# Low parts of the projections' weights by an adding transfer instead of a subtraction

## The chip, the cores and the metric

The kernel runs on one core of a Trainium2 chip. The metric is the device time of one execution in microseconds; the time of a kernel is the median of its runs. The core has five engines that work side by side, each with its own queue of instructions in a fixed order: TensorE (PE, matmuls; PEld is its loading of weights), VectorE (DVE), ScalarE (ACT), GpSimd (POOL) and SyncE (SP, which only issues transfers here). Transfers (DMA) between HBM and the on-chip memory are issued from SP, ACT or POOL and carried out by 16 transfer engines. An instruction waits in its queue until the semaphores it needs are set, and everything behind it waits too.

## The reference

Two layers on a sequence of 1024 tokens of width 1024, all in float32. The first layer is a mixer followed by a mixture of experts, the second one is attention and pooling followed by a gated network. The change lies in the mixer's input projection:

```
h = rmsnorm(x, norm_g)
proj = h @ w_in                      # 1024 x 1024 by 1024 x 2048
y_hyena = hyena_mixer(proj[..., :1536], ...)     # short convolution, long convolution by FFT
y_fourier = fourier_mixer(proj[..., 1536:])
y = head_rmsnorm(concatenate([y_hyena, y_fourier]), mix_g)
x = x + y @ w_out
```

## The kernel before

**Matrix products in three parts.** TensorE multiplies in a rounded float32 (`F32R`). To keep the accuracy, each operand is split into a high part, the value rounded by writing it as `F32R`, and a low part, the value less the high part. `mm3` then issues three matmuls into one PSUM tile: high by high (L61), high by low (L62) and low by high (L64). `split` makes the parts: ScalarE casts (L51), VectorE subtracts (L52).

**The input projection.** `w_in` is cut into 16 column tiles of 128 outputs, each 128 partitions by 8 by 128 values (4 KB per partition, 512 KB). `weight(c)` loads tile `c` into `wr` by a transfer from SP (L110) and splits it into `wh` and `wl`. The pool `pw` has two buffers of each of these, so a tile can be loaded and split while TensorE works on the one before, and a split into a buffer waits until the matmuls of the tile two before are done. `proj(c)` runs 48 matmuls per tile: two halves of 512 tokens, 8 pieces of the inner dimension, three matmuls each. The third matmul of each piece needs `wl`. Its outputs are PSUM tiles named `proj` (or `tp`, for the tile that is called with `pair`).

**Order of the stage.** The tiles come in the order 12, 13, 14, 15 (the Fourier half, `proj_u`, whose results are scaled on VectorE at L181), then 4, 8, 5, 9, then 6, 10, 7, 11, then 0, 1, 2, 3 (`conv`). Tile 12 is loaded and split first of all, between the pieces of the input `x`, which `split` with a scale turns into `xh` (L54) and `xl` (L55). Between the projections stand: the filter's small network (`mlp`, L298, L304), the norm (matmuls with `ones`, L165), the filter's spectrum (`filter_spectrum`, twice, GpSimd's part of it at L408), the data's spectrum (`data_spectrum`, twice) and its product with the filter (`filtered`, twice; VectorE at L542 to L547, GpSimd at L543 and L544, loads of `K` from SP at L540). `conv` scales the projection from PSUM into `up` on VectorE (L197), which also frees the PSUM tile for a later projection, and does the short convolution on ScalarE (L198) and VectorE (L199, L200). GpSimd clears two columns of `up` (L194, L195).

**GpSimd's transfers.** GpSimd issues, early on, four transfers of 1 MB, the transform constants `fwh` and `fwl` (L150). They are held back until the input has landed: a copy of two values of the last piece of `x` into each of the two tiles stands ahead of them (L148).

The instructions of an engine don't stand strictly in the order of the source: the framework that builds the kernel puts them in an order by their place in the source and by when it takes them to be ready.

Of the kernel before, what the change touches and what calls it, by code (L numbers as in the profile page):

```python
# [13 lines left out]
AF = mybir.ActivationFunctionType  # L14
# [4 lines left out]
MUL, ADD, SUB = ALU.mult, ALU.add, ALU.subtract  # L19
# [25 lines left out]
def f32(ap):  # L45
    return ap.bitcast(F32)

def split(nc, hi, lo, src, scale=None):

    if scale is None:  # L50
        nc.scalar.copy(hi, src)  # L51
        nc.vector.tensor_sub(lo, src, f32(hi))  # L52
    else:
        nc.scalar.activation(hi, src, AF.Copy, scale=scale)  # L54
        nc.vector.scalar_tensor_tensor(lo, src, scale, f32(hi), op0=MUL, op1=SUB)  # L55
# [27 lines left out]
def mixer(g):  # L83
    nc, tc, I = g.nc, g.tc, g.I
# [23 lines left out]
    def weight(c):  # L108
        wr = pw.tile([P, 8, P], F32, name="wr", tag="wr")
        nc.sync.dma_start(out=wr, in_=I["w_in"][c])  # L110
        wh = pw.tile([P, 8, P], F32R, name="wh")
        wl = pw.tile([P, 8, P], F32R, name="wl")
        split(nc, wh, wl, wr)
        return wh, wl

    def proj(c, w=None, pair=False):
        wh, wl = w or weight(c)
        if pair:
            both = ps.tile([P, 2, 512], F32, name="tp")
        out = []  # L120
        for h in range(2):
            sl = slice(h * 512, h * 512 + 512)
            pt = both[:, h] if pair else psA.tile([P, 512], F32, name="proj")
            for k in range(8):
                mm3(nc, [pt], wh[:, k], wl[:, k], [xh[k][:, sl]], [xl[k][:, sl]], k == 0, k == 7)
            out.append((pt, sl))
        return out

    keep_warm(g, psA.tile([P, 4, P], F32, name="proj"), g.ones, g.ones[:, None, :].to_broadcast([P, 4, P]), 5)
    with tpool(tc, name="kst", bufs=2) as pk:  # L130
# [11 lines left out]
        xs = x_in(0)  # L142
        xs = [next(xs), xs]
        w12 = weight(12)
        xs = [xs[0], *xs[1], *x_in(4)]
        for t, nm in ((g.fwh, "c_fwh"), (g.fwl, "c_fwl")):

            nc.gpsimd.tensor_copy(t[0:1, 0, :, 0, 0], xs[3][0:1, 1, 0:2])  # L148
            for q in range(2):
                nc.gpsimd.dma_start(out=t[:, :, q].rearrange("p r a b -> p r (a b)"),  # L150
                                    in_=I[nm][:, q].rearrange("r p c -> p r c"))
# [1995 lines left out]
```

## Time and profile before

| | us |
|---|---|
| median of 3 runs | 2517.74 |
| lowest and highest run | 2515.53, 2522.01 |
| the profiled execution, its own time | 2524.19 |
| its span, first to last instruction | 2522.4 |

The profile is of one execution. Its times count from the start of the span. In the page the busy time of an engine is given with its share of the span. A line of a timeline gives start, duration, engine, line of the kernel, operation, tiles and shapes; the square brackets at its end say how long the engine had been idle before it, and what ended that. Matmuls are pipelined, and their ends are modelled: the distance between two starts says more than the duration. The granted clock of TensorE (PEclk) was 0.978 of full speed in the mean.

### The profile page before, as it was taken

What the parts mean: (1) busy time and instruction counts of PE and PEld (TensorE: products, weight loads), DVE (VectorE), ACT (ScalarE), POOL (GpSimd) and SP (SyncE); (2) the same over time, 40 slices, a digit from 0 to 9 for tenths busy, and PEclk for the clock granted to TensorE, in tenths of its full rate; (3) what the DMA queues carried; (4) which work ended last, traced back from release to release, by engine and by line L of the source; (5) the groups of instructions that cost most, each with busy time, mean ns of one, the idle gap of its engine ahead of it and who ended that gap; (6) DMA issues with size and microseconds to landing.
All of it is one profiled execution on the core that took longest, in us unless ns stands there. A gap on an engine that the chain in (4) does not pass through costs nothing.

```text
span 2522.4 us, 30742 instructions
## 1 busy us (share of the span) xinstructions
PE 2396.0 (95%) x11367; PEld 1885.5 (75%) x11367; DVE 1783.4 (71%) x2440; ACT 1288.8 (51%) x1702; POOL 596.7 (24%) x552
## 2 busy tenths in 40 slices
PE   9999688989999999997999999998989999999998
PEld 6887575867777777766888777776878888887786
DVE  7757686459999998886512665666488787777666
ACT  6322145337777777776312765662354444444443
POOL 1124442122222223412101011101113443442001
PEclk9999898989999999998999999998999999999999
DMA  6313645279999999965122111126213322326765
GB/s 230 120 57 127 211 140 207 107 255 368 371 368 370 371 363 358 361 237 198 34 76 97 55 42 53 61 67 233 82 70 101 109 105 92 113 97 235 229 199 184
DMA packets 121666, 451.16 MB, mean 179 GB/s; under 512 B 17510, under 2 KB 20520, under 8 KB 95658
## 3 DMA queue, kind: packets, MB, share of 16 engines
q1 hardware_dynamic: 87136, 346.94, 38.6%
q0 software_dynamic: 31776, 100.73, 12.2%
q8 instruction: 90, 1.47, 0.2%
q10 hardware_dynamic: 2602, 1.51, 0.2%
q14 instruction: 62, 0.51, 0.1%
HBM read 382.79 MB, written 74.71 MB: 181 GB/s over the span
## 4 chain that ended last, share of the span: by engine, by line
PE 70%; DVE 6%; ACT 4%; issue 3%; DMA 2%; POOL 1%; SPq 0%; DVEq 0%; POOLq 0%; ACTq 0%
PE proj L61 12%; PE proj L64 11%; PE proj L62 11%; PE w_gate L62 2%; PE w_up L61 2%; PE w_up L62 2%; PE w_up L64 2%; PE w_gate L64 2%; PE w_gate L61 2%; PE yd L61 2%; PE yd L62 2%; PE yd L64 2%; PE pmix L64 1%; PE pmix L61 1%; PE pmix L62 1%
## 5 line engine op out<-in xcount | busy, mean ns | idle before, releaser
L1000 DVE TENSOR_TENSOR wlo<-raw,whi 128x2048 fp32r<-128x2048 f32 (+1 forms) x195 | 438.6, 2255 | 47.5 <-ACT whi L999 43.6
L999 ACT CAST whi<-raw 128x2048 fp32r<-128x2048 f32 (+1 forms) x195 | 365.6, 1880 | 74.2 <-PE w_up L64 29.5
L61 PE MATMUL proj<-hh,wthi 128*128 128x512 f32 (+1 forms) x576 | 214.3, 376 | 1.3 <-ACT wthi L51 0.9
L62 PE MATMUL proj<-hl,wthi 128*128 128x512 f32 (+1 forms) x576 | 215.3, 375 | 0.2
L64 PE MATMUL proj<-hh,wtlo 128*128 128x512 f32 (+1 forms) x576 | 214.5, 374 | 0.0
L1058 POOL DMA_INDIRECT x1d<-y,tab x32 | 105.9, 3310 | 229.6 <-ACT whi L999 173.7
L52 DVE TENSOR_TENSOR wtlo<-wraw,wthi 128x1024 fp32r<-128x1024 f32 (+1 forms) x44 | 49.5, 1126 | 130.1 <-ACT wthi L51 129.7
L1751 POOL TENSOR_TENSOR vg<-vg 128x1024 f32<-128x1024 f32 x22 | 66.5, 3025 | 258.9 <-ACT vg L1750 258.9
L62 PE MATMUL proj<-fdbl,fdah 128*128 128x512 f32 x308 | 121.9, 396 | 4.5 <-DVE fdbl L52 4.4
L61 PE MATMUL proj<-fdbh,fdah 128*128 128x512 f32 x308 | 121.6, 395 | 3.7 <-DVE fo L1872 2.9
L61 PEld LDWEIGHTS proj<-hh,wthi 128*128 128x128 f32 x576 | 108.3, 190 | 19.2 <-ACT wthi L51 1.3
L62 PEld LDWEIGHTS proj<-hl,wthi 128*128 128x128 f32 x576 | 108.7, 189 | 17.9 <-DVE hl L52 0.7
L64 PEld LDWEIGHTS proj<-hh,wtlo 128*128 128x128 f32 x576 | 108.7, 189 | 17.3
L64 PE MATMUL proj<-fdbh,fdal 128*128 128x512 f32 x308 | 121.0, 393 | 0.0
L61 PE MATMUL proj<-xh,wh 128*128 128x512 f32 x240 | 96.9, 405 | 11.5 <-DVE up L197 10.6
L62 PE MATMUL w_gate<-wlo,xh 128*96 128x512 f32 x256 | 102.0, 398 | 2.4 <-DVE wlo L1000 2.3
L77 POOL TENSOR_TENSOR rs_o<-rs_v,mhalf 128x1 f32<-128x1 f32 x48 | 38.2, 796 | 271.0 <-DVE ssf L1869 178.6
L62 PE MATMUL w_up<-wlo,xh 128*96 128x512 f32 x256 | 101.2, 395 | 0.0
L61 PE MATMUL w_gate<-whi,xh 128*96 128x512 f32 x256 | 100.9, 394 | 0.2
L61 PE MATMUL w_up<-whi,xh 128*96 128x512 f32 x256 | 100.9, 394 | 0.0
L64 PE MATMUL w_gate<-whi,xl 128*96 128x512 f32 x256 | 100.6, 393 | 0.0
L64 PE MATMUL w_up<-whi,xl 128*96 128x512 f32 x256 | 100.5, 392 | 0.0
(544 smaller groups left out, 6781.9 us busy)
## 6 DMA issues: line engine op xcount, KB each, us to landing
raw<-in_w_gate SPq DMA_DIRECT2D x64, 1024.0 KB, 19.1
raw<-in_w_down SPq DMA_DIRECT2D x63, 1024.0 KB, 21.5
raw<-in_w_up SPq DMA_DIRECT2D x62, 1024.0 KB, 21.5
wraw<-in_w_up SPq DMA_DIRECT2D x44, 512.0 KB, 3.5
draw<-in_w_down SPq DMA_DIRECT2D x88, 256.0 KB, 3.7
draw<-ad SPq DMA_DIRECT2D x77, 256.0 KB, 2.8
wraw<-in_w_in SPq DMA_DIRECT2D x32, 512.0 KB, 3.6
ad<-as POOLq DMA_DIRECT2D x44, 256.0 KB, 2.3
```

The lines of the kernel that those rows point to most:

```text
L52: nc.vector.tensor_sub(lo, src, f32(hi))
L61: nc.tensor.matmul(outs[i], lhsT=wh, rhs=xh[i], start=start, stop=False, skip_group_check=onto)
L62: nc.tensor.matmul(outs[i], lhsT=wh, rhs=xl[i], start=False, stop=False, skip_group_check=onto)
L64: nc.tensor.matmul(outs[i], lhsT=wl, rhs=xh[i], start=False, stop=stop, skip_group_check=onto)
L77: nc.gpsimd.tensor_tensor(o, v, g.mhalf if n == 1 else g.mhalf.to_broadcast([P, n]), op=ALU.pow)
L999: g.nc.scalar.copy(hi[:, sl], raw[:, sl])
L1000: eng.tensor_sub(lo[:, sl], raw[:, sl], f32(hi[:, sl]))
L1058: return nc.gpsimd.indirect_dma_start(out=g.x1d, out_offset=bass.IndirectOffsetOnAxis(ap=rows, axis=0), in_=y.rearrange("p a b -> p (a b)" ...
L1751: nc.gpsimd.tensor_mul(va, va, ga)
```

## The change

In `weight(c)` the split stays as it is for tile 12. For the 15 other tiles the high part is made by the same cast on ScalarE, and the low part in two steps: ScalarE writes the negated weights into `wl`, rounded as the high part is, and then a transfer issued from GpSimd reads the raw weights from HBM again and adds them to what stands in `wl`. The sum is the raw value less the high part.

```
         wh = pw.tile([P, 8, P], F32R, name="wh")
         wl = pw.tile([P, 8, P], F32R, name="wl")
-        split(nc, wh, wl, wr)
+        if c == 12:
+            split(nc, wh, wl, wr)
+        else:
+
+            nc.scalar.copy(wh, wr)
+            nc.scalar.activation(wl, wr, AF.Copy, scale=-1.0)
+            nc.gpsimd.dma_start(out=wl, in_=I["w_in"][c], accum_op=ADD)
         return wh, wl
```

## Rows read from the trace of the kernel before

**Rows 1.** The page: busy time by engine; the last chain's shares by engine.
```profile
PE 2396.0 (95%) x11367; PEld 1885.5 (75%) x11367; DVE 1783.4 (71%) x2440; ACT 1288.8 (51%) x1702; POOL 596.7 (24%) x552
...
PE 70%; DVE 6%; ACT 4%; issue 3%; DMA 2%; POOL 1%; SPq 0%; DVEq 0%; POOLq 0%; ACTq 0%
```

**Rows 2.** Windows: length, busy PE, PEld, DVE, ACT, POOL; PEclk, DMA share, GB/s.
```profile
30.00:45.00 15.00, 15.00 (x63) 11.53 (x62) 10.69 (x23) 12.09 (x17) 0.00 (x0) 1.00 0.76 235
45.00:120.00 75.00, 74.72 (x461) 66.05 (x460) 60.87 (x115) 27.33 (x48) 7.73 (x6) 1.00 0.36 124
120.00:160.00 40.00, 40.00 (x178) 32.40 (x178) 22.57 (x21) 9.28 (x9) 7.18 (x9) 1.00 0.27 92
```

**Rows 3.** Waits of PE, 30 to 160 us: total us, times, longest.
```profile
PE hp L370 <- ACT fwoh L51: 0.2, 1, 0.2
```

**Rows 4.** Waits of PE, 180 to 290 us.
```profile
PE proj L61 <- DVE up L197: 10.6, 7, 3.7
```

**Rows 5.** Tile view of wh: ns min/median/max, first and last start us.
```profile
L51 ACT CAST wh<-wr x16: 1029/1047/1057, 9.7 to 258.6; 128x1024 fp32r<-128x1024 f32 x16
L52 DVE TENSOR_TENSOR wl<-wr,wh x16: 1215/1221/1719, 11.6 to 268.0; 128x1024 fp32r<-128x1024 f32 x16
```

**Rows 6.** Tile view of wl, 180 to 290 us.
```profile
L52 DVE TENSOR_TENSOR wl<-wr,wh x6: 1215/1218/1719, 187.3 to 268.0; 128x1024 fp32r<-128x1024 f32 x6
```

**Rows 7.** Timeline of VectorE, 186 to 196 us.
```profile
194.74 0.68 DVE L197 TENSOR_TENSOR up<-proj,rb 128x512 f32<-128x512 f32 x1
```

**Rows 8.** Timeline of ScalarE, 0 to 130 us.
```profile
21.89 1.13 ACT L54 ACTIVATE xh<-xr,g 128x1024 fp32r<-128x1024 f32 x1
...
24.94 1.03 ACT L51 CAST wh<-wr 128x1024 fp32r<-128x1024 f32 x1
...
28.88 1.03 ACT L51 CAST wh<-wr 128x1024 fp32r<-128x1024 f32 x1
```

**Rows 9.** DMA view: issues by line, KB each, median us from issue to landing.
```profile
wr<-in_w_in SPq DMA_DIRECT2D x16, 512.0 KB, 4.0
...
xb<-h2d,tab POOLq DMA_INDIRECT x32, 9.0
x1d<-y,tab POOLq DMA_INDIRECT x32, 10.5
```

**Rows 10.** Timeline of ScalarE, 125 to 320 us.
```profile
132.53 1.06 ACT L51 CAST wh<-wr 128x1024 fp32r<-128x1024 f32 x1 [8.76 <-PE proj L62]
133.50 1.25 ACT L198 ACTIVATE vc<-up,cw 128x1024 f32<-128x1024 f32 x1
```

**Rows 11.** Timeline of TensorE, 140 to 150 us.
```profile
144.23 0.40 PE L64 MATMUL proj<-xh,wl 128*128 128x512 f32 x1
```

**Rows 12.** Tile views of fwh and fwl: the constants' issues and landings.
```profile
L150 POOL DMA_DIRECT2D fwh<-in_c_fwh x2: 778/849/920, 21.5 to 22.5; - x2
...
DMA to landing us min/median/max: 5.8/6.7/7.6
...
L150 POOL DMA_DIRECT2D fwl<-in_c_fwl x2: 775/778/782, 23.2 to 23.9; - x2
...
DMA to landing us min/median/max: 9.9/12.0/14.1
```

**Rows 13.** Timeline of TensorE, 27 to 35 us.
```profile
29.92 0.39 PE L64 MATMUL tp<-xh,wl 128*128 128x512 f32 x1
30.15 0.39 PE L61 MATMUL tp<-xh,wh 128*128 128x512 f32 x1
...
32.48 1.88 PE L165 MATMUL tp<-xr,ones 128*128 128x512 f32 x4
```

**Rows 14.** Timeline of TensorE, 268 to 273 us.
```profile
268.13 0.50 PE L61 MATMUL proj<-xh,wh 128*128 128x512 f32 x1 [3.74 <-DVE up L197]
...
269.23 0.63 PE L62 MATMUL proj<-xl,wh 128*128 128x512 f32 x1
...
271.79 0.63 PE L62 MATMUL proj<-xl,wh 128*128 128x512 f32 x1
```

## The prediction

> **What bounds the kernel now.** The page first: TensorE is busy 95% of the span and carries 70% of the chain that ended last [rows 1]. The shares of that chain add up to 86%, since it isn't followed back to the start; the missing 14%, some 350 us, are the beginning, with the stage that the diff touches (the mixer's projections, 0 to 290 us). I therefore read that stage by its windows and waits. From 30 to 160 us TensorE has work in 129.7 of 130 us [rows 2], and its waits in these 130 us come to 0.2 us [rows 3]. So here a stall of TensorE is not made up later: every microsecond moves all that follows. From 180 to 290 us it is different: there TensorE waits seven times, 10.6 us in all, for VectorE's `up` (L197), which empties a projection's PSUM bank [rows 4]. VectorE is a candidate for a gain there, and there alone.
>
> **What is removed.** Fifteen of the sixteen subtractions `wl <- wr, wh` on VectorE, 1.22 us each [rows 5]: 18.3 us. From 30 to 160 us TensorE waits for none of VectorE's work, so there the removal is worth nothing; the cover is TensorE's own stream of matmuls. From 180 to 290 us it counts where a subtraction stands in VectorE's queue ahead of an L197 for which TensorE waits. Six of the fifteen fall there (column tiles 7, 11 and 0 to 3), the first at 187.3 us [rows 6], ahead of the L197 at 194.74 [rows 7]. Not every one precedes a wait, and in between VectorE waits for transfers and for GpSimd, which swallows the time. Bounds: nothing, and all 10.6 us. I take two subtractions' worth, a gain of 2 us, nearer the low end because six subtractions are 7.3 us at the most.
>
> **What is added on ScalarE.** Fifteen negated copies, between 1.05 us (the cast of a weight [rows 5]) and 1.13 us (an activation with a scale on the same shape [rows 8]): 16 us. ScalarE is busy 27 of 75 us from 45 to 120 and 9 of 40 after [rows 2], so there it costs nothing but latency: the low part begins a copy later. In the first 45 us ScalarE is nearly full, and two copies push the squares and the filter's sines back by 1 us each; TensorE's own stream covers that from 30 us on, and I put it at zero (bounds 0 and 2).
>
> **What is added as transfers.** Fifteen transfers of 512 KB from HBM, adding into `wl`, issued from GpSimd. A low part was there after 1.05 us of cast and 1.22 us of subtraction; it now needs the cast, the negation, GpSimd's turn and a whole transfer. The trace shows no adding transfer into SBUF. Nearest rows: a plain load of the same 512 KB lands in 4.0 us; the adding scatter of 384 KB into HBM (L1058, 96 rows of 4 KB) lands in 10.5, where the gather of as much lands in 9.0 under the same traffic [rows 9]. So the adding itself is worth some 1.5 us, and a landing lies between 4.0 and 10.5; I take 5.5, near the plain load, since the gather shows where most of the scatter's time comes from.
>
> **Most loads have room for it.** A weight is loaded while TensorE still works on the one before. Column tile 8 is typical of the tight ones: cast at 132.53 [rows 10], first use of the low part at 144.23 [rows 11], a lead of 11.7 us. Needed: 1.05 + 1.13, another 1.25 if the convolution's activation goes between [rows 10], and 5.5 from issue to landing: 7.7 to 8.9 us. It fits with 3 us in hand. Some issues will meet GpSimd in a long operation ahead of them in its queue; and while an issue waits for its negation, GpSimd's own work stands behind it (the products of L543 and L544, for whose results VectorE's L546 and then L197 wait). For both together I add 1 us (lower bound 0). That the raw tile `wr` now comes free at the negation and not at the subtraction moves the next plain load by about nothing, and the 7.9 MB read a second time find transfer engines that are 27 to 36% busy from 45 to 160 us [rows 2]. The upper bound is the scatter's 10.5: 12.7 to 13.9 us, late by 1.0 to 2.2 us on each of about six loads with a lead like this, say 9 us.
>
> **The second load has none.** This is column tile 13, the first of the fifteen. Its cast starts at 24.94 [rows 8], so the negation is done at 27.0 at the earliest, and near 30 if it falls where the next weight's cast was (28.88). GpSimd's queue is the trouble: just ahead, at 21.5 to 23.9 us, it issues four transfers of 1 MB, the constants fwh and fwl. Start and time to landing [rows 12] give landings at 21.5 + 5.8 = 27.3, then 22.5 + 7.6 = 30.1, 23.2 + 9.9 = 33.1 and 23.9 + 14.1 = 38.0 us: one behind the other, 2.8 to 4.9 us per MB, 3.6 in the mean. The new transfer stands behind them in the same queue, so its 0.5 MB lands at 38.0 + 1.8 = 39.8 at best, and with the adding's 1.5 at 41.3; I take 41.0 (upper bound 43, if it moves its bytes twice as well). TensorE wants this low part at 29.92 [rows 13]. Behind that matmul in its queue stand the rest of the tile's 48 and then all of the filter's. The stall is 41.0 - 29.92 = 11.1 us.
>
> What could be done in the meantime: the four matmuls for the norm at 32.48 (1.88 us [rows 13]), if they are put ahead of the waiting one: a credit of 0 to 1.9, I take 1.0. And the clock: after a wait of 3.74 us at 268.13, the seven matmuls from 269.23 to 271.79 start 0.43 us apart [rows 14], where 0.23 is usual at the full clock (29.92 to 30.15 [rows 13]): 1.4 us lost. A wait of 11 us should lose no less: 1.5.
>
> By the Trainium skill's page "DMA: Bandwidth & Descriptors", section on the anatomy of one DMA on the SWDGE (gpsimd) path, a transfer takes about 2.0 us plus its bytes by 436 GB/s, an estimate of 3.2 us for 512 KB; from an issue at 27 to 30 us that would leave a stall of under 4 us. The constants' four transfers here don't agree with it: it gives 4.4 us for 1 MB, and they took 5.8 to 14.1.
> The Trainium skill's page "Collectives: The Full Stack", where it explains why ReduceScatter is half of AllGather, says that an add in the transfer's path needs two source reads per byte delivered; by that the 1.8 us would be 3.6, the landing 41.6 and the sum 0.6 larger, an estimate. No row here shows it for SBUF.
>
> **Sum.** 11.1 - 1.0 + 1.5 for the second load, + 1.0 for the others, - 2.0 for VectorE: + 10.6 us. The profiled execution took 2524.19 us (span 2522.4), 6.5 above the median of the runs, 2517.74; the difference goes on the median: 2528 us. About 0.3% (7.6 us) is what can be told from no change here.
>
> **The rivals.**
> A (forecast): the second low part waits behind the constants. Own range: a stall of 9.9 less 1.9 of credit, less 4 on VectorE, gives + 4; 13.1 + 1.5 + 2 gives + 17: 2522 to 2535.
> B, the transfer is hidden anyway: it lands some 5 us after its issue because the transfer engines take it between the constants' pieces, or because it is issued ahead of them, at about 32 us. Stall 2, VectorE 2 back: 2518. For it: the order in which a queue's pieces run on the engines isn't in the rows, only the landings are. Against: those four come strictly in order of issue.
> C, adding is slow everywhere: at the scatter's 10.5 us each tight load is late too, + 11 and 9 more: 2538. For it: the only adding rows. Against: the gather beside it is nearly as slow, so most of it is traffic, which this stage has less of.
> D, VectorE's queue was the bound from 180 on: without the subtractions each L197 comes before TensorE asks, and the 10.6 us vanish. It decides once the stall at the second load is under 10.6; with one of 2 it gives - 8.6, 2509 us. For it: seven waits with one releaser [rows 4]. Against: six subtractions hold 7.3 us of VectorE, not 10.6.
>
> **How the numbers follow.** A 0.56, B 0.22, C 0.14, D 0.08. Of A, some 0.44 lies above + 7.6 us; with C that is 0.58 slower; the rest of A and B, 0.34, is no difference; D, 0.08, is faster. The range reaches from D's upper part to C: 2512 to 2541.
>
> **What would show it.** Right: TensorE's first `xh,wl` matmul of the second tile near 41 instead of 29.92 us with a wait of about 10 us for the transfer into `wl`, a low clock right after, and everything from 45 to 160 us unchanged but moved. The adding transfers issued later land in 5 to 6 us, and TensorE doesn't wait for them. The seven waits for L197 shrink by about 2 us. Wrong: the second transfer landing before 35 us, or its constants issued behind it; or waits for `wl` at six or more tiles.

## The result, and the profile after

The changed kernel takes 2551.98 us (median of 4 runs, 2548.36 to 2557.0), the kernel before beside it 2517.53: a ratio of 1.0125, interval 1.0109 to 1.0142. The forecast was 2528 with a range that ended at 2541, so the time lies outside it, on the side that was forecast. The profiled execution took 2551.96 us, its span is 2550.2 (before: 2522.4). In the lines below, those behind the edit have moved by six: the cast is L117, the negation L118, the adding transfer L119, and `up` is L203 instead of L197.

The page's busy times by engine first; they answer to [rows 1]:

```profile
PE 2393.4 (94%) x11367; PEld 1883.9 (74%) x11367; DVE 1760.8 (69%) x2425; ACT 1303.4 (51%) x1717; POOL 606.3 (24%) x567
```

VectorE's 15 subtractions are gone (2440 to 2425 instructions), ScalarE has 15 copies more, TensorE's work is the same. The loss is waiting. The windows that answer to [rows 2], with the same columns:

```profile
30.00:45.00 15.00, 7.13 (x18) 4.81 (x19) 8.02 (x19) 12.77 (x18) 1.80 (x2) 0.71 1.08 300
45.00:120.00 75.00, 69.06 (x377) 58.56 (x377) 50.73 (x99) 29.29 (x48) 7.65 (x7) 0.97 0.41 122
120.00:160.00 40.00, 40.00 (x226) 34.68 (x225) 16.70 (x25) 9.22 (x11) 9.43 (x11) 1.00 0.51 134
```

TensorE was busy for 15.00, 74.72 and 40.00 us in these stretches [rows 2]; it now has 7.13, 69.06 and 40.00. The waits of TensorE from 30 to 160 us (engine, line, what it waited for: total us, times, longest), which came to 0.2 us [rows 3]:

```profile
PE tp L64 <- DMA wl<-in_w_in: 6.9, 1, 6.9
PE hp L376 <- DVE eo L388: 2.5, 1, 2.5
PE hp L376 <- DVE fwol L52: 2.2, 1, 2.2
PE hp L376 <- ACT fwoh L51: 1.2, 1, 1.2
PE tp L171 <- DVE xr L169: 1.1, 1, 1.1
```

The first is the second load, as forecast. The next three were not: TensorE waits for the filter's spectrum (`hp`), which has no part in the change. From 180 to 290 us, against 10.6 us in seven waits [rows 4]:

```profile
PE proj L61 <- DVE up L203: 7.7, 3, 4.5
PE proj L64 <- DMA wl<-in_w_in: 2.4, 2, 1.3
```

**The second load.** The timelines of TensorE, and of GpSimd ahead of it, at column tile 13:

```profile
40.72 0.79 PE L64 MATMUL tp<-xh,wl 128*128 128x512 f32 x1 [6.87 <-DMA wl<-in_w_in]
42.16 0.63 PE L64 MATMUL tp<-xh,wl 128*128 128x512 f32 x1
...
46.00 0.63 PE L64 MATMUL tp<-xh,wl 128*128 128x512 f32 x1
...
46.98 0.39 PE L64 MATMUL tp<-xh,wl 128*128 128x512 f32 x1
```

```profile
23.03 1.52 POOL L156 DMA_DIRECT2D fwl<-in_c_fwl  x2
30.04 0.93 POOL L119 DMA_DIRECT2D wl<-in_w_in  x1 [5.50 <-DVE my L306]
```

The first low-part matmul starts at 40.72 instead of 29.92 [rows 13]: 10.8 us late, where 11.1 was forecast. Of these TensorE waits only 6.87 in one piece, because the norm's matmuls and some of the network's went ahead. After it the matmuls are 0.43 us apart (from 42.16 to 46.00 nine starts) until about 46.7; the granted clock is 0.50 of full speed from 40.7 to 46.4 (1.2 of 2.4 GHz). (The issue at 30.04 waited for the negated copy, which ends at 29.74; the line names another instruction that ended at about that time, and in the run with tile 13 alone it names the copy.)

**Landings.** Issues of transfers by line, KB each, median us from issue to landing; `wr` had 4.0 [rows 9]:

```profile
wr<-in_w_in SPq DMA_DIRECT2D x16, 512.0 KB, 5.6
wl<-in_w_in POOLq DMA_DIRECT2D x15, 512.0 KB, 8.0
```

An adding transfer lands in 8.0 us, not in 5.5, and the plain load beside it has become slower by 1.6.

**Column tile 2.** A stall as long as the second load's, which the forecast did not have. GpSimd's and then TensorE's timeline:

```profile
272.10 0.58 POOL L562 DMA_DIRECT2D iwl<-in_c_iwl  x1
282.46 1.69 POOL L549 TENSOR_TENSOR pp<-Ys,K 128x512 f32<-128x512 f32 x1 [9.79 <-DMA K<-kd]
284.13 1.70 POOL L550 TENSOR_TENSOR pp<-Yc,K 128x512 f32<-128x512 f32 x1
...
286.42 1.81 POOL L119 DMA_DIRECT2D wl<-in_w_in  x2
```

```profile
295.62 0.80 PE L64 MATMUL proj<-xh,wl 128*128 128x512 f32 x1 [10.71 <-DMA wl<-in_w_in]
```

GpSimd waits 9.79 us for a load of `K`; the low part of tile 2 is issued behind the two products that need it, and TensorE waits 10.71 us.

**Where the 30 us are.** A landmark measures each stage better than the end: the start of the same matmul in both traces. Tile 13's first low part is 10.8 us late, tiles 8, 5, 9, 6 and 10 are 18.5 late, tiles 0 and 1 19.9, and the experts' first matmul, which has everything of the mixer behind it, starts at 584.9 instead of 554.6:

```profile
L61 PEld LDWEIGHTS w_gate<-whi,xh x256: 159/162/165, 584.9 to 1146.0; 128*96 128x96 f32 x128
```

That is 30.3 us; at 1158 us it is still 30.1. So there are three losses: some 11 at the second load, 7.5 in the filter's stage (45 to 120 us), and 12 between there and the experts.

### The profile page after: what moved, and what is told of

The parts are those of the page before. It is cut to its first block, busy times and chain, and to the rows that moved or that the text cites. A ratio compares the mean times of both kernels' runs of the same rounds, so it can differ in the third digit from the quotient of the medians.

```text
span 2550.2 us, 30774 instructions
## 1 busy us (share of the span) xinstructions
PE 2393.4 (94%) x11367; PEld 1883.9 (74%) x11367; DVE 1760.8 (69%) x2425; ACT 1303.4 (51%) x1717; POOL 606.3 (24%) x567
## 4 chain that ended last, share of the span: by engine, by line
PE 65%; DVE 6%; ACT 4%; issue 3%; DMA 3%; POOL 1%; SPq 0%; DVEq 0%; POOLq 0%; ACTq 0%
PE proj L61 11%; PE proj L64 10%; PE proj L62 10%; PE w_gate L62 2%; PE w_up L62 2%; PE w_up L61 2%; PE w_up L64 2%; PE w_gate L64 2%; PE w_gate L61 2%; PE yd L61 2%; PE yd L62 2%; PE yd L64 2%; DMA draw<-in_w_down 2%; PE pmix L61 1%; PE pmix L64 1%
## 5 line engine op out<-in xcount | busy, mean ns | idle before, releaser
L62 PEld LDWEIGHTS proj<-hl,wthi 128*128 128x128 f32 x576 | 108.8, 189 | 17.9 <-DVE hl L52 0.8
L64 PE MATMUL proj<-xh,wl 128*128 128x512 f32 x240 | 97.0, 405 | 13.5 <-DMA wl<-in_w_in 13.1
```

Source lines behind the costliest of these rows:

```text
L62: nc.tensor.matmul(outs[i], lhsT=wh, rhs=xl[i], start=False, stop=False, skip_group_check=onto)
L64: nc.tensor.matmul(outs[i], lhsT=wl, rhs=xh[i], start=False, stop=stop, skip_group_check=onto)
```

## The experiments

Each run is compared with the kernel before on the same chip. The table gives, beside the ratio, how late TensorE is against the profile before at the first low part of tile 8 (121.83 us there), of tile 1 (247.89), and at the experts' first matmul (554.6). The ratio counts the rest of the kernel too, where executions of one program differ by some us; the last column does not, but it is read from one execution, and the mixer can differ between executions too.

| what adds | median us | before | ratio, interval | tile 8 | tile 1 | experts |
|---|---|---|---|---|---|---|
| all 15 (the change) | 2551.98 | 2517.53 | 1.0125, 1.0109 to 1.0142 | +18.5 | +19.9 | +30.3 |
| all but 13 | 2548.55 | 2523.33 | 1.0113, 1.0087 to 1.0138 | +8.9 | +11.3 | +21.9 |
| 13 | 2534.07 | 2523.33 | 1.0045, 1.0031 to 1.0059 | +12.4 | +12.1 | +11.4 |
| all but 2 | 2556.22 | 2523.33 | 1.0134, 1.0112 to 1.0157 | +18.7 | +22.8 | +29.8 |
| all but 13 and 2 | 2544.12 | 2523.33 | 1.0087, 1.0065 to 1.0109 | +9.0 | +11.7 | +21.7 |
| all, plain transfer | 2550.09 | 2520.71 | 1.0110, 1.0093 to 1.0127 | +15.5 | +16.9 | +27.3 |
| all, 13 ahead of the constants | 2555.33 | 2520.71 | 1.0134, 1.0117 to 1.0151 | +14.8 | +17.9 | +29.5 |
| 14, 15, 4 | 2523.93 | 2520.71 | 1.0008, 0.9998 to 1.0017 | +2.9 | +2.9 | +2.0 |
| none, copies only | 2525.57 | 2520.71 | 1.0013, 0.9999 to 1.0027 | +0.7 | +1.1 | +5.9 |
| 14, 15, 4, 8 | 2536.80 | 2520.86 | 1.0064, 1.0040 to 1.0089 | +9.0 | +8.8 | +8.6 |
| 5, 9, 6, 10 | 2524.26 | 2520.86 | 1.0011, 1.0000 to 1.0023 | -0.7 | +1.9 | -0.1 |
| 7, 11 | 2523.99 | 2520.56 | 1.0012, 1.0002 to 1.0022 | -0.9 | +4.5 | +2.2 |
| 0, 1, 3 | 2528.89 | 2522.30 | 1.0040, 1.0025 to 1.0054 | +0.1 | +0.1 | +2.2 |
| 7, 11, 0, 1, 3 | 2531.97 | 2520.56 | 1.0039, 1.0024 to 1.0054 | -0.9 | +3.6 | +10.6 |
| 2 | 2533.54 | 2522.30 | 1.0048, 1.0031 to 1.0065 | -0.7 | -0.5 | +9.4 |
| 0, 1, 2, 3 | 2533.66 | 2520.86 | 1.0047, 1.0030 to 1.0064 | -0.6 | -0.4 | +8.3 |

**The second load, with and without.** Two edits of one condition: tile 13 keeps its subtraction, or it alone adds.

```
-        if c == 12:
+        if c in (12, 13):
```

> Tile 13 keeps the subtraction, 14 tiles use the adding transfer. Theory: the loss has three places: the second load behind the constants (about 12 us), the filter's stage between 55 and 140 us, whose small loads are slowed by the adding transfers beside them (about 6.5), and tile 2's transfer behind a waiting product in GpSimd's queue (about 10). Then only the 12 go: some 19 us slower than before remain, TensorE waits for no wl before 45 us, and the filter's stage still loses time. Rival 1: the loss in the filter's stage is only what the late second tile left behind; then it goes too, and some 13 us remain. Rival 2: the loss is spread over all transfers; then 28 us remain.

```
-        if c == 12:
+        if c != 13:
```

> Only tile 13 uses the adding transfer, 15 tiles keep the subtraction. Theory: its stall alone, 11 to 12 us slower than before, first use of its low part near 41 us. Rival 1 (the filter's stage suffers from the late second tile): 18 us slower. Rival 2 (the loss is spread over all transfers): 2 to 4 us slower.

Alone, tile 13 costs 11.4 us at the experts and 2534.07 us. That is the forecast's first term, as it was worked out. But without it the other fourteen still cost 21.9, and the tiles from 8 on are 8.9 us late though tile 13 is on time. So the filter's loss is no echo of the late second load, and the forecast's + 1.0 for the others is where it went wrong.

**Tile 2's stall, taken away.**

```
-        if c == 12:
+        if c in (12, 2):
```

> Tile 2 keeps the subtraction, 14 tiles use the adding transfer. Theory: the stall of 10.7 us at tile 2 goes and what followed it, some 21 us slower than before remain. Rival: tile 2 would have waited there anyway for VectorE's up (before the change it waited 3.7 us there), or tile 3, whose transfer was issued in the same moment, now waits as long; then 27 to 30 us remain.

```
-        if c == 12:
+        if c in (12, 13, 2):
```

> Tiles 13 and 2 keep the subtraction, 13 tiles use the adding transfer. Theory: what is left is the filter's stage and small waits at tiles 7 and 11, 7 to 9 us slower than before. Rival 1 (the filter's stage suffered from the late second tile only): 0 to 3 us slower. Rival 3: without the two long stalls the 13 saved subtractions show as a gain of 2 to 4 us.

The wait of 10.7 us is gone in both, and the experts start 29.8 and 21.7 us late, against 30.3 and 21.9 with it. A wait of 10 us removed, 0.5 and 0.2 us won: something else ends just as late.

**Is it the adding?** The same transfers, the same waits and bytes, without the add.

```
-            nc.gpsimd.dma_start(out=wl, in_=I["w_in"][c], accum_op=ADD)
+            nc.gpsimd.dma_start(out=wl, in_=I["w_in"][c])
```

> The fifteen second transfers keep their place, waits, bytes and queue, but overwrite the low part with the raw weights instead of adding to it, so only the adding is taken out of the timing (the low parts hold the raw weights). Theory (the adding holds the transfer engines): a plain transfer lands in 4 to 5.5 us instead of 8.0, the small loads beside it go back to 2.2 to 4 us, the filter stage (45 to 130 us) loses 2 us or less instead of 6.5, tile 13 starts its low part at 37 to 39 us; first expert matmul +13 to +20, 2531 to 2540 us. Rival (the second read of 7.9 MB is what costs, adding or not): landings stay at 7 to 8 us, 2546 to 2555 us.

The time (2550.09) is the rival's, the landings are nearer to the theory's. The issues by line in this run:

```profile
wr<-in_w_in SPq DMA_DIRECT2D x16, 512.0 KB, 4.6
wl<-in_w_in POOLq DMA_DIRECT2D x15, 512.0 KB, 5.9
```

A plain transfer lands in 5.9 us instead of 8.0, near the 5.5 that the forecast took, and still 27.3 of the 30.3 us are lost. The adding itself costs 3. By the rule of two source reads per delivered byte in the Trainium skill's "Collectives: The Full Stack" (where it explains why ReduceScatter is half of AllGather) the add would lengthen a landing by 1.8 us, an estimate from the 3.6 us per MB of the constants [rows 12]; the two medians differ by 2.1, which agrees with it, and it hardly matters for the sum.

**Is it VectorE's and ScalarE's work?** Cast and negation, no transfer, no subtraction.

```
-            nc.gpsimd.dma_start(out=wl, in_=I["w_in"][c], accum_op=ADD)
```

> Cast and negation on ScalarE for fifteen tiles, no subtraction and no second transfer (the low parts hold the negative high parts): what VectorE's relief is worth and the negation costs with no transfer. Theory: TensorE's waits for L203 between 180 and 290 us shrink by 2 to 4 of their 10.6 us, nothing else changes; -1 to -4, 2519 to 2522 us. Rival (VectorE's queue was the bound there): the waits nearly vanish, -7 to -10, 2513 to 2516 us. Second rival (the order of the tail takes it back): waits shrink, first expert matmul within 1 us of before.

Fifteen subtractions less on VectorE, and TensorE's waits for `up` (here L202) from 180 to 290 us are what they were, 10.6 [rows 4]:

```profile
PE proj L61 <- DVE up L202: 10.3, 4, 6.4
```

The relief, net of ScalarE's copies, is worth nothing; the experts' 5.9 us speak for a small loss in the tail, the time (1.0013, interval 0.9999 to 1.0027) can't tell it from none. The theory and both rivals fall: they all had these waits shrink. Beside the plain transfers' run this one shows that the second reads bring tile 8's 15.5 us nearly alone (0.7 without them).

**The queue.** Tile 13's transfer ahead of the constants: a gate reads its negated low part.

```
+        w13 = weight(13, lambda w: nc.gpsimd.tensor_copy(rb[0:1, 0:2], w[0:1, 0, 0:2]))
         for t, nm in ((g.fwh, "c_fwh"), (g.fwl, "c_fwl")):
-
-            nc.gpsimd.tensor_copy(t[0:1, 0, :, 0, 0], xs[3][0:1, 1, 0:2])
+            nc.gpsimd.tensor_copy(t[0:1, 0, :, 0, 0], rb[0:1, 0:2])
```

> All fifteen add, but tile 13's adding transfer stands in GpSimd's queue ahead of the four transfers of the constants fwh and fwl. Theory (one behind the other in the queue): it is issued at 27 to 28 us and lands 6 to 8 us later, first low part matmul of tile 13 at 34 to 36 instead of 40.7, so the stall is 4 to 6 us; the constants land 6 to 8 us later, which costs up to 2 at the filter's first use of them; 2544 to 2549 us. Rival (the four MB share the 16 engines with it whatever the order): first low part matmul stays at 39 to 42, 2550 to 2556 us.

GpSimd's and TensorE's timelines in this run (the transfer is L121), and the negated copy of tile 13 on ScalarE, first in this run and then in the change:

```profile
24.59 1.08 POOL L121 DMA_DIRECT2D wl<-in_w_in  x1 [0.32 <-POOL rb L154]
...
26.02 1.57 POOL L158 DMA_DIRECT2D fwh<-in_c_fwh  x2 [0.20 <-POOL fwl L156]
```

```profile
30.27 0.79 PE L64 MATMUL tp<-xh,wl 128*128 128x512 f32 x1 [4.02 <-DMA wl<-in_w_in]
```

```profile
21.44 1.06 ACT L118 ACTIVATE wl<-wr 128x1024 fp32r<-128x1024 f32 x1
```

```profile
28.70 1.04 ACT L118 ACTIVATE wl<-wr 128x1024 fp32r<-128x1024 f32 x1
```

It lands within 5.7 us of its issue, ahead of the 4 MB that were issued 1.4 us later, where behind them it took 10.7 (30.04 to 40.72), and the tile ends 5.3 us late instead of 11.0; the rival falls. The edit did more than turn the order of the queue, though: tile 13's cast and negation moved forward as well. Of the 10.4 us by which its first low part is earlier, 5.4 are the earlier issue and 5.0 the shorter landing. And of the 5.7 us gained at the tile's end 3.7 are left at tile 8 and 0.8 at the experts, and the time shows none of it.

**The filter's stage.** First three tiles whose transfers run beside the filter's loads, then tile 8 in addition.

```
-        if c == 12:
+        if c not in (14, 15, 4):
```

> Only tiles 14, 15 and 4 add, the ones whose transfers run while the filter's small loads do; the 13 others keep the subtraction. Theory (the adding transfers slow the loads beside them): dec, fwo and ud beside them land in 5 to 6 us instead of 2.2 to 2.8, and the tiles from 8 on start 7 to 10 us later than before although tile 13 is on time; first expert matmul +7 to +11, 2529 to 2535 us. Rival (the filter stage's loss comes from its work being put in another order when all fifteen add, or from the late tile 13): tiles from 8 on +0 to +3, 2521 to 2527 us.

```
-        if c == 12:
+        if c not in (14, 15, 4, 8):
```

> Tiles 14, 15, 4 and 8 add: the run with 14, 15 and 4, and tile 8 in addition. Theory (tile 8's second load and its plain load go out at 100 us just ahead of a load of 128 KB, dec, for the filter's second half, which then lands in 7 us instead of 2 and holds up TensorE by 4 and the clock after it): tiles from 8 on start 8 to 9.5 us later than before instead of 2.9; first expert matmul +6 to +10. Rival (the filter's loss needs tiles 5 to 3 as well, by the order of the whole stage): 2 to 4 us at tile 8.

Three cost 2.9 us at tile 8 and no measurable time: as a general tax on small loads, the theory falls (the stores of `u` beside them do land in 7.0 us instead of 2.3, but that costs nothing measurable). With tile 8 it is 9.0, as expected. The timelines of SP, GpSimd, VectorE and TensorE in the run with tile 8:

```profile
97.88 0.33 SPq L110 DMA_DIRECT2D wr<-in_w_in  x1
98.75 0.33 SPq L387 DMA_DIRECT2D dec<-in_c_dec  x1
```

```profile
98.15 0.88 POOL L119 DMA_DIRECT2D wl<-in_w_in  x1 [14.37 <-ACT wl L118]
```

```profile
107.18 0.69 DVE L388 TENSOR_TENSOR eo<-hp,dec 128x512 f32<-128x512 f32 x1 [5.67 <-DMA dec<-in_c_dec]
```

```profile
108.58 0.58 PE L61 MATMUL tp<-kh,fwh 128*128 128x256 f32 x1 [4.95 <-ACT kh L51]
```

And VectorE's line for the same `eo` in the run without tile 8, where `dec` goes out at 99.93:

```profile
102.96 0.68 DVE L388 TENSOR_TENSOR eo<-hp,dec 128x512 f32<-128x512 f32 x1
```

A plain load and tile 8's second read go out 0.9 and 0.6 us ahead of a small `dec` load, the last of the filter's second half. (The plain load is tile 9's, the eighth in order; it goes out as soon as tile 8's negated copy frees the buffer.) VectorE has `dec` 8.4 us after its issue (98.75 to 107.18), against at most 3.0 without them (99.93 to 102.96). ScalarE's cast of `kh` and TensorE's transform stand behind it: a wait of 4.95, and the low clock after it (0.83 granted from 100 to 120 us, 1.00 without tile 8). The plain load alone doesn't do it: in the run with the copies only it goes out 0.5 us ahead of a `dec`, which VectorE has 3.5 us after its issue. The timelines of SP and VectorE there:

```profile
95.35 0.33 SPq L110 DMA_DIRECT2D wr<-in_w_in  x1
95.87 0.33 SPq L386 DMA_DIRECT2D dec<-in_c_dec  x1
```

```profile
99.40 0.69 DVE L387 TENSOR_TENSOR eo<-hp,dec 128x512 f32<-128x512 f32 x1 [0.42 <-DMA dec<-in_c_dec]
```

One transfer in the wrong place costs 6 us; it was not the low part that came too late, but a neighbour.

The run with all but 13 has the same collision (VectorE waits 4.6 us for that `dec`). In the change itself it doesn't occur: with tile 13 late, tile 8's second read goes out only at 117.59, behind the last `dec` (112.37). The same happens there to another `dec`, behind tile 15's second read. The timelines of GpSimd, SP, VectorE and TensorE in the change:

```profile
56.49 0.86 POOL L119 DMA_DIRECT2D wl<-in_w_in  x1 [23.69 <-ACT wl L118]
```

```profile
56.63 0.39 SPq L110 DMA_DIRECT2D wr<-in_w_in  x1
57.73 0.33 SPq L387 DMA_DIRECT2D dec<-in_c_dec  x1
...
112.37 0.33 SPq L387 DMA_DIRECT2D dec<-in_c_dec  x1
```

```profile
64.50 0.69 DVE L388 TENSOR_TENSOR eo<-hp,dec 128x512 f32<-128x512 f32 x1 [2.80 <-DMA dec<-in_c_dec]
```

```profile
65.24 0.49 PE L376 MATMUL hp<-fweh,H 128*128 128x512 f32 x1 [2.54 <-DVE eo L388]
```

That is 2.5 of the 7.5 us. Another 3.4 are TensorE's two waits for the parts of `fwo`; this load lands in 3.0 us (2.7 before) but goes out at 91.47, 8 us later than before (83.44). Why TensorE has no other work in that stretch stays open.

**Loads with room.**

```
-        if c == 12:
+        if c not in (5, 9, 6, 10):
```

> Tiles 5, 9, 6 and 10 add, those that are loaded while TensorE has a plain stream of projections and no small load is beside them. Theory (a second load costs nothing by itself where the buffer is free early and nothing else is asked of the transfer engines): no wait of TensorE for the low parts, tiles from 5 on within 1 us of before, first expert matmul within 2 us, 2517 to 2523 us. Rival (every adding transfer costs 1 us or more): +4 or more at tile 7, 2525 us or more.

Here the forecast's argument holds in the main: nothing at the experts, at most 2.0 us on the way, and one wait for a low part, of 1.3 us. The time, 2524.26 us, lies just above what was expected; the ratio's interval reaches from nothing to 0.2%, so a small price is not excluded.

**The tail.** Two halves of the rest, and then the pieces of the last four.

```
-        if c == 12:
+        if c not in (0, 1, 2, 3):
```

> Only tiles 0 to 3 add, the last four; everything up to 200 us is as in the kernel before. Theory (a loss of its own in the tail: tile 2's transfer stands in GpSimd's queue behind the products that wait for K, and what TensorE does not get done there is done after the first y load): a wait of about 10 us at tile 2's first low part, first expert matmul +7 to +11, 2529 to 2533 us. Rival (the tail lost only because the stages ahead of it were late): first expert matmul within 3 us of before, 2519 to 2524 us, whatever tile 2 waits for.

```
+        if c not in (2,):
```

> Only tile 2 adds, the one whose transfer stands in GpSimd's queue behind the products that wait for K. Theory (the tail's 8 us come from tile 2's stall): a wait of 8 to 11 us at its first low part, first expert matmul +6 to +9, 2528 to 2531 us. Rival (the second reads of 0, 1 and 3 slow the K loads and the y loads): first expert matmul +0 to +3.

```
+        if c not in (0, 1, 3):
```

> Tiles 0, 1 and 3 add, tile 2 is split: the other side of the run with tile 2 alone. Theory (tile 2's stall is the tail's price): first expert matmul within 2 us of before, 2519 to 2524 us. Rival (K and y loads are slowed by 0, 1 and 3): +5 to +9, 2526 to 2531 us.

```
+        if c not in (7, 11):
```

> Only tiles 7 and 11 add, the last two groups not tried by themselves; their transfers run beside the K loads of the first product with the filter. Theory (second reads beside the K loads cost a little, by a later K): first expert matmul +1 to +3, 2520 to 2525 us. Rival (these two are what the runs with tile 2 split lost behind tile 1): first expert matmul +6 to +10.

```
+        if c not in (7, 11, 0, 1, 3):
```

> Tiles 7, 11, 0, 1 and 3 add, tile 2 is split: the second half of the run in which 12, 13 and 2 were split, with nothing ahead of it. Theory (what that run lost behind tile 1, 10 us at the first expert matmul, is a matter of these five): tile 1 +2 to +4, first expert matmul +9 to +13. Rival (it needs the late stages ahead of it, so that the order of the tail is another one): tile 1 +0 to +4, first expert matmul +2 to +5.

Tile 2 alone costs 9.4 us at the experts (its wait is 6.5 us there, and 11.3 with 0, 1 and 3 beside it), the five others together 10.6. So the tail can lose its 10 us in two ways, by tile 2's stall or by the five others, and the two don't add up, which fits that splitting tile 2 gave nothing back.

What the five's parts cost is less sure. The last column has 2.2 us for 7 and 11 and 2.2 for 0, 1 and 3, but the execution that was profiled was the fastest of five for 0, 1 and 3 (2522.22 us, the others 2527.62 to 2534.07) and the slowest of six for the five. Behind the experts' first matmul all 20 traces take 1962 to 1972 us, so the execution of 2534.07 us will have lost more than 2.2 ahead of it. By the times, 0, 1 and 3 cost 6.6 us (the ratio's interval says 6 to 14, as the rival had it), 7 and 11 3.4, and the five 11.4, which is about their sum. How the five lose it: TensorE's waits from 180 to 290 us in that run, then VectorE's and TensorE's timelines.

```profile
PE proj L61 <- DVE up L203: 15.0, 5, 6.4
```

```profile
206.15 0.69 DVE L548 TENSOR_TENSOR pp<-Yc,K 128x512 f32<-128x512 f32 x1 [1.80 <-DMA K<-kd]
206.76 2.30 DVE L206 SCALAR_TENSOR_TENSOR vc<-up,cw,vc 128x1024 f32<-128x1024 f32 x1
208.98 1.75 DVE L551 TENSOR_TENSOR pp<-Ys,K 128x512 f32<-128x512 f32 x1
210.65 0.68 DVE L203 TENSOR_TENSOR up<-proj,rb 128x512 f32<-128x512 f32 x1
```

```profile
211.47 0.76 PE L61 MATMUL proj<-xh,wh 128*128 128x512 f32 x1 [4.26 <-DVE up L203]
```

VectorE has one subtraction left there (tile 2's), and instead stands in front of the product with `K`; its waits for `K` from 184 to 300 us grew from 8.5 to 15.9 us, with the `up` for which TensorE waits (15.0 us, before 10.6) queued behind. These 4.4 us are what the waits show; TensorE's first low part of tile 3, the last tile, is 4.2 late, and the other 6 us are lost behind it.

**Orders and buffers of the tail.** Three more runs on what sets its end: the kernel before with two buffers for `K`, the same with the second `y` and `s` loads tied behind a load of `uf`, and tiles 0 to 3 adding with that tie.

```
-        K = pool.tile([P, 2, 512], F32, name="K", bufs=1)
+        K = pool.tile([P, 2, 512], F32, name="K", bufs=2)
```

> The kernel before with two buffers for K instead of one, no adding transfer: a look at what sets the tail, 190 to 310 us. Theory (the chain of K load, products, next K load sets the first y load, and the y load sets the end of the mixer): each K load after the first is hidden, the first y load goes out 6 to 12 us earlier, first expert matmul 4 to 10 us earlier, 2508 to 2516 us. Rival (VectorE's and TensorE's work sets it): within 2 us, 2516 to 2522 us.

```
+    if hh == 1:
+        nc.gpsimd.tensor_copy(y[0:1, 0, 0:1], g.uf[1][0:1, 0:1])
     nc.sync.dma_start(out=y, in_=g.yd[hh, 0])
```

> The kernel before with two buffers for K, and the second pair of y and s loads tied behind the second load of uf by two copies of one value, so that the Fourier half's loads stand first in SP's queue. Theory (with two K buffers alone the first y load went out 9 us earlier, but uf went out 16 us later, behind the s load): uf goes out at 290 to 293 us, TensorE's wait for uh goes away, first expert matmul 3 to 8 us earlier than before, 2512 to 2518 us. Rival (the end of the mixer is TensorE's and VectorE's work, not these loads): within 2 us of before.

> Tiles 0 to 3 add, with the same tie of y and s behind uf: the tail's run with another order in SP's queue. Theory (tile 2's stall of 11 us is made up for the most part, and the 8 us come from the uf loads that stand behind the s load in SP's queue, 25 us late): uf goes out at 299 to 302 us instead of 315, first expert matmul +2 to +5 instead of +8.3. Rival (the stall itself is what is lost): first expert matmul +7 to +10, whatever the order.

All three theories fell in what they say of the time. With two buffers the first `y` load goes out at 274.7 instead of 283.9 us, and the experts start 3.2 us later (ratio 1.0012, interval 0.9999 to 1.0024); with the tie it goes out at 273.7 and they start 0.4 earlier (1.0003, 0.9994 to 1.0013). With tile 2's stall, `uf` at 298.4 us instead of 315.1 changes nothing (9.5 us late at the experts, 2533.38 us, 1.0051, 1.0035 to 1.0068). So moving those loads forward does not move the end of the mixer, and none of these versions is faster than the kernel before.

## Why the prediction was wrong

**Right: the second load.** The stall of 11.1 us measured 10.8, and the run with tile 13 alone 11.4 at the experts, where stall, credit and clock together were put at 11.6. The reason holds too: behind the constants in GpSimd's queue the transfer took 10.7 us from its issue, ahead of them 5.7. Only the share of the adding was smaller there: 0.7 us, not 1.5 (40.07 with the plain transfer). The sentence on the Trainium skill's "DMA: Bandwidth & Descriptors" (anatomy of one DMA on the SWDGE (gpsimd) path) gave 3.2 us for such a transfer, an estimate; the run with plain transfers doesn't agree with it, its fastest landing took 4.4. Rival B falls.

**The step that failed: "For both together I add 1 us".** It is in the part "Most loads have room for it", and it is the whole price of the fourteen other tiles in the sum. They cost 21.9 us, and the thirteen without tile 2 21.7. The groups, each by itself, cost 8.6 (14, 15, 4, 8), nothing (5, 9, 6, 10) and 10.6 (7, 11, 0, 1, 3); with 11.4 for tile 13 that makes 30.5, against 30.3 measured. That the two meet is partly chance: tile 2 is left out, the collision that costs the first group 6 us isn't in the change, where tile 13 is late, and by the median times the same four runs add up to 41.5 against 34.5.

What failed was not the landing that went into the step. It was taken as 5.5 and measured 8.0, inside its bounds; but with plain transfers, which landed in 5.9, nearly the same time was lost. The step asked only whether TensorE gets each low part in time, and it mostly does. It did not ask who else waits: a small `dec` load behind large ones (2.5 us in the change, 6 at tile 8 where tile 13 is on time), and `K` for VectorE. The upper bound, "late by 1.0 to 2.2 us on each of about six loads", asked the same wrong question, so the range was too narrow. The products of L543 and L544 and the `up` behind them were named there and got their price in the same 1 us; the waits for `up` alone grew by 4.4 us in the run with the five. Tile 2, whose issue stands behind a product that waits 9.8 us, was the issue that "will meet GpSimd in a long operation".

**A wrong name.** The tile with the cast at 132.53 and the low part at 144.23, "column tile 8" in the prediction, is the eighth in order, and that is tile 9. Tile 8 is cast at 88.11 and used at 121.83. The lead of 11.7 us is that of the tiles inside a plain stream of projections, for which the argument held; tile 8, whose second read does the harm, stands beside the filter's loads.

**- 2.0 for VectorE: it measured 0.** In the copies' run VectorE waits 12.6 us for `K` from 184 to 300 us, where it waited 8.5, and TensorE's waits for `up` stay what they were. That run has the relief and ScalarE's copies together, so 0 is the net of both. Rival D falls with it, and "ScalarE 0" stands within the 0.7 us of the copies' run at tile 8.

**Rival C** came near in size (2538) by another mechanism: it had the adding make every tight load late, and the adding is worth 3 us.

**The signs given.** Held: tile 13 near 41 with the low clock behind it. Not held: 45 to 160 us "unchanged but moved" (TensorE loses 5.7 busy us from 45 to 120), landings of 5 to 6, no wait for later low parts (tile 2). The waits for `up` shrank as said, from 10.6 to 7.7 us, but not by the relief: in the copies' run they are 10.3. The sign for wrong, waits at six or more tiles, did not appear either: in the mixer's whole stage TensorE waits for `wl` at four places.

**Open.** Where the five tiles of the tail lose the part of their 10.6 us that comes behind tile 3, what ends the mixer once tile 2's stall is away, and what makes up the rest of the filter's 7.5 us in the change, was not settled; the waits for `K` are shown, but with two `K` buffers the kernel before was no faster.

## What to carry to other kernels

A second transfer of the same data is not free because its own reader can wait: find out which small, just-in-time loads go out right behind it, and what stands behind its issue in the issuing queue. Work that was taken off VectorE, which waits for a transfer, gave nothing back here. And where several stalls lie in one stage, take them away together in a test before their prices are added: here 9.4 and 10.6 made 11.8 behind tile 8 in the change.

## What had not been expected of the hardware

An adding transfer of 512 KB into on-chip memory landed in 8.0 us (median of 15), the same transfer without the add in 5.9; GpSimd was held for 0.87 us by the issue of an adding one and 0.55 by a plain one. A small `dec` load with two transfers of 512 KB issued 0.6 and 0.9 us ahead of it, one of them adding, was there after 8.4 us, where 2.0 is usual; with the plain one alone ahead of it, after 3.5.
